# Spreading products over all 128 rows instead of 12 or 16, in a chain of two transformer blocks

## The chip, the cores and the metric

The kernel runs on one core of one Trainium2 chip, as one program in one launch. The metric is device microseconds from start to end, the median of several executions. Without the change it is 3619.73 us, the median of 3 runs (3617.62 to 3626.06).

## What is computed

Two blocks follow one another on 256 tokens of width 1024 (272 with 16 learned ones in the first block). The first block has two layers, each a SwiGLU network, a mixer and another SwiGLU network; the mixer of its first layer (the "first mixer") joins attention with a forget gate and a gated delta rule, that of its second layer is a recurrence (RWKV-7). The second block has attention, a gated linear recurrence and a retrieval layer; the change does not touch it. What matters of the reference:

```python
def forgetting_attention(q, k, v, log_f):
    c = jnp.cumsum(log_f, axis=-1)
    ...
        logits = jnp.einsum('bhqd,bhkd->bhqk', qb, k) * scale + cb[..., :, None] - c[..., None, :]
    ...
def gated_delta_rule(q, k, v, log_g, beta):
    gc = jnp.cumsum(log_g.reshape(B_, H, nc, CHUNK), axis=-1)
    decay = jnp.exp(jnp.where(causal, gc[..., :, None] - gc[..., None, :], -jnp.inf))
    kb = k * beta[..., None]
    ...
    q_dec = q * egc
    ...
def rwkv7_time_mix(h, ...):
    ...
    kk = l2_normalize((k * k_k).reshape(B_, L, H, N))
    y = rwkv7_recurrence(r_h, decay, k_h, v_h, -kk, kk * a_h)
    ...
    bonus = jnp.sum(r_h * k_h * r_k.astype(f32), axis=-1, keepdims=True) * v_h
```

Each has numbers that there are one of per head and token (the summed gates, the norms' factors, the bonus sums), and that must be applied to all the features of a head, which lie over the partitions.

## The kernel before, in words

Activations lie feature by feature over the partitions, tokens along the free axis (T = 272, in tiles of 16, 128 and 128 tokens). A weight or an activation is split into a high and a low part of a 32-bit format that TensorE takes quickly (`wload`, L77, loads through SP's DMA queue, casts `wh` on ACT at L89 and subtracts `wl` on DVE at L90), and each dense product is three (`mm3`, L114: lines L116 to L118).

A number per head and token is computed as a row, one partition per head, and is spread over the 128 partitions by a product with a selector, a matrix of zeros with ones in one row: `bcast` (L418 in the first mixer, L1064 in the recurrence) issues two, for the row's high and low part. The selectors come from an array of constants that already has 128 rows, those below the used ones zero. These are the products in question, named by the tiles that they read:

- `decay` (L517): `rowh`, `rowl` (12 rows, the summed gates) with the selector `selr`, one pair per head, 4 in all, lines L419 and L420. The rows are made in `sums` (L485).
- `scaled` (L587): `frh`, `frl` (16 rows: four factors of four heads, made in `frows`, L576), four pairs per head, 16 in all, the same lines. DVE multiplies each with keys or queries (L591).
- `attend` (L804): for each of 8 heads and 3 tiles of queries a pair that adds the keys' summed gates to the logits (L819, L820), behind products of the queries with the keys over 64 rows (L813) and one that adds the causal mask over as many rows as the tile has tokens (L815).
- In the recurrence `rows_split` (L1057) makes `rrh`, `rrl` (16 rows: the inverse norms of the keys, from `rsqrt` on DVE, L171 to L176), spread in `first` (L1271) and `unit` (L1306); `bsum` and `bsul` (16 rows, the bonus sums) are spread in `finish` (L1486). The selector there is `e2r`.

TensorE's products run in the order in which they are issued. That order follows from the generators: in the dense part of the first mixer small steps are put behind the n-th next weight block (`after`, L101, and `tick`, L105); later steps of the chains, of attention heads and of dense products take turns (`round`, L984). DVE, ACT and POOL each run theirs in order too.

Of the kernel before, what the change touches and what calls it, by code (L numbers as in the profile page):

```python
# [10 lines left out]
F32R = mybir.dt.float32r  # L11
# [321 lines left out]
class Block1(Core):  # L333
# [48 lines left out]
    def _hybrid(self, ctx, h, g):  # L382
# [15 lines left out]
        idb = ht([P, P], "idb", BF16)  # L398
        selr = ht([16, 16 * P], "selr", F32R)

        def select(q):
            w = self.wp.tile([P, 1024], F32, name=nm("w"), tag="w", bufs=WB)
            o = COFF["sel"][0] + q * 1024
            nc.sync.dma_start(w[:16], a["consts"][:16, o : o + 1024])
            V.tensor_copy(selr[:, q * 1024 : (q + 1) * 1024], w[:16])

# [10 lines left out]

        def bcast(p, rh, rl, j, n):  # L418
            M(p, selr[:n, j * P : j * P + P], rh, start=True, stop=False)  # L419
            M(p, selr[:n, j * P : j * P + P], rl, start=False, stop=True)  # L420

# [23 lines left out]
        cols, lg = ht([P, 3, 12], "cols"), ht([P, 3, 12], "lg")  # L445
        row, rowh, rowl = ht([12, T], "row"), ht([12, T], "rowh", F32R), ht([12, T], "rowl", F32R)
        em = [ht([P, 4, n], f"em{i}") for i, (_, n) in enumerate(TILES)]
# [37 lines left out]
        def sums():  # L485

            for i, (t0, n) in enumerate(TILES):
                p = psm()
                M(p[:12, :n], lg[:n, i], tri[:n, :n], start=True, stop=True)
                V.tensor_copy(row[:, t0 : t0 + n], p[:12, :n])  # L490
            c = ht([8, T], "t16")
            V.tensor_scalar(c[:, :16], row[:8, :16], -1.0, None, op0=OP.mult)
            for i in (1, 2):
                t0, n = TILES[i]
                V.tensor_scalar(c[:, t0 : t0 + n], row[:8, t0 : t0 + n], -1.0, c[:, t0 - 1 : t0], op0=OP.mult, op1=OP.add)
            V.tensor_copy(row[:8], c)
            S.copy(rowh, row)
            V.tensor_tensor(rowl, row, rowh, op=OP.subtract)
            G.memset(egc, 1.0)
            after(1, tokens)  # L500
# [16 lines left out]
        def decay(hd):  # L517

            p = psm()
            bcast(p[:, :T], rowh, rowl, 8 + hd, 12)  # L520
            for i, (t0, n) in enumerate(TILES):
                S.activation(em[i][:n, hd], p[:n, t0 : t0 + n], AF.Relu, scale=-1.0, bias=cols[:n, i, 8 + hd : 9 + hd])
            if hd == 3:
                for i, (t0, n) in enumerate(TILES):
                    S.activation(em[i][:n], em[i][:n], AF.Exp, scale=-1.0)
                    G.tensor_tensor(em[i][:n], em[i][:n], tri[:n, :n].unsqueeze(1).to_broadcast([n, 4, n]), op=OP.mult)
# [33 lines left out]

        frh, frl = ht([16, T], "frh", F32R), ht([16, T], "frl", F32R)

        def factors():
# [12 lines left out]
        def frows(fac):  # L576
            p = psm()
            for i, (t0, n) in enumerate(TILES):
                TR(p[:16, t0 : t0 + n], fac[:n, i].rearrange("p a b -> p (a b)"), ident[:n, :n])
            S.copy(frh, p[:16, :T])  # L580
            V.tensor_tensor(frl, p[:16, :T], frh, op=OP.subtract)
            for hd in range(4):
                after(1 + hd, lambda hd=hd: scaled(hd))
# [3 lines left out]
        def scaled(hd):  # L587
            for f, dst, src in ((3, kb, raw[1]), (2, kn, raw[1]), (0, qq, raw[0]), (1, qd, raw[0])):
                p = psm()
                bcast(p[:, :T], frh, frl, f * 4 + hd, 16)  # L590
                V.tensor_tensor(dst[:, hd], src[:, hd], p[:, :T], op=OP.mult)  # L591
# [212 lines left out]
        def attend(j, i):  # L804
# [11 lines left out]
            for q, p in enumerate(ps):  # L816
                hd = 2 * j + q
                s = selr[:12, hd * P : hd * P + n]
                M(p, s, rowh[:, :nk], start=False, stop=False)  # L819
# [199 lines left out]
    def _rwkv(self, ctx, h, g):  # L1019
# [16 lines left out]
        e2 = self.konst(op_, "e2")  # L1036
        e2r = ot([16, 8 * P], "e2r", F32R)
        w = self.wp.tile([P, 1024], F32, name=nm("w"), tag="w", bufs=WB)
        o = COFF["e2t"][0]
        nc.sync.dma_start(w[:16], a["consts"][:16, o : o + 1024])  # L1040
        V.tensor_copy(e2r, w[:16])

# [11 lines left out]
        gl = ot([P, 2, NT], "gl", F32R)  # L1054
        bsum = [ot([16, NT], "bsum", F32R), ot([16, NT], "bsul", F32R)]

        def rows_split(src, n):  # L1057
            x = ot([16, T], "rrh", F32R)[:, :n]
            y = ot([16, T], "rrl", F32R)[:, :n]
            S.copy(x, src)  # L1060
# [20 lines left out]
        with ExitStack() as c1:  # L1081
# [109 lines left out]
            for m in range(KT):  # L1191
# [39 lines left out]
                M(pn[:48, NM:T], e2[:, m * 80 : m * 80 + 48], rk, start=False, stop=m == KT - 1)  # L1231
            ns, rs, rt = t1([65, T], "th")[:16], t1([P, T], "ksq")[:16], t1([P, T], "kt")[:16]
            V.tensor_scalar(ns, pn[:16, :T], 1e-6, None, op0=OP.add)
            S.copy(bsum[0], pn[32:48, NM:T])
            V.tensor_tensor(bsum[1], pn[32:48, NM:T], bsum[0], op=OP.subtract)
            xv = mix(3, True)
            self.rsqrt(rs, ns, rt)
            rh, rl = rows_split(rs, T)


# [1247 lines left out]
```

## Time and profile before

| | us |
|---|---|
| median of 3 runs | 3619.73 |
| the profiled execution | 3625.6 |
| its span, first to last instruction | 3623.8 |
| PE (matmuls) busy | 3534.2 (98%) |
| PEld (weight loads) busy | 3356.2 (93%) |
| DVE busy | 2755.6 (76%) |
| ACT busy | 1932.1 (53%) |
| POOL busy | 291.8 (8%) |

PE is TensorE's matmul, PEld its load of the stationary operand, DVE VectorE, ACT ScalarE, POOL GpSimd, SP the engine whose queue issues the transfers. A form such as `12*128 12x272` is a product over 12 rows, with 128 columns of the stationary operand and 272 of the moving one. "Granted clock" is the share of TensorE's full clock, 1.00 or 0.50; its mean over the span is 0.980. Matmuls overlap, so busy PE is not PE at its peak; the distance from the start of one to the start of the next tells the pace. The first mixer runs from about 217 to 440 us, the recurrence from about 857 to 1190.

### The profile page before, as it was taken

The page shows a single profiled execution, that of the slowest core. Times are in us where ns is not written, and L with a number is a line of the kernel's source. Part 1 is how long each engine was busy: PE and PEld are TensorE (multiplying, and loading weights), DVE is VectorE, ACT ScalarE, POOL GpSimd, SP SyncE. Part 2 cuts the span into 40 slices and gives each one's busy share as a digit, 9 for nine tenths or more (in the row PEclk, how much of TensorE's full clock was granted, in tenths as well). Part 3 has the DMA queues.
Part 4 walks back from the last instruction along what each step waited for, and adds up shares of the span by engine and source line. Part 5 has one row for each costly group of instructions (what it writes and reads, how often), then busy time and mean ns, then how long its engine had stood idle before and what let it go on. Part 6 is the DMA issues. An engine that isn't in the chain of part 4 may idle for free. (4 is left out here: it accounts for less than half of the span.)

```text
span 3623.8 us, 79395 instructions
## 1 busy us (share of the span) xinstructions
PE 3534.2 (98%) x31065; PEld 3356.2 (93%) x31065; DVE 2755.6 (76%) x6245; ACT 1932.1 (53%) x4109; POOL 291.8 (8%) x380
## 2 busy tenths in 40 slices
PE   8999999999998999999999999999999999999998
PEld 8998899998887999989999999999989999997887
DVE  6677676667866877788997788657778997778866
ACT  5553455555632556655554454556765555455554
POOL 2121021110200100011000000001011000000000
PEclk9999899999997999999999999999999999999999
DMA  5551155554300565445555555555435555555554
GB/s 182 173 160 63 64 171 175 172 172 130 109 24 25 192 183 177 135 145 171 175 181 172 168 168 169 175 185 163 152 129 175 174 172 179 170 169 182 174 187 151
DMA packets 160581, 560.95 MB, mean 155 GB/s; under 512 B 18954, under 2 KB 21402, under 8 KB 160204
## 3 DMA queue, kind: packets, MB, share of 16 engines
q1 hardware_dynamic: 159788, 554.55, 47.0%
q8 instruction: 243, 3.98, 0.5%
q0 software_dynamic: 416, 1.32, 0.1%
q14 instruction: 134, 1.10, 0.1%
HBM read 554.75 MB, written 1.05 MB: 153 GB/s over the span
## 5 line engine op out<-in xcount | busy, mean ns | idle before, releaser
L89 ACT CAST wh<-w 128x512 fp32r<-128x512 f32 (+1 forms) x2102 | 1292.1, 617 | 1220.0 <-PE mm L117 723.8
L90 DVE TENSOR_TENSOR wl<-w,wh 128x512 fp32r<-128x512 f32 (+1 forms) x2102 | 1459.3, 699 | 561.2 <-ACT wh L89 530.4
L116 PE MATMUL mm<-xh,wh 128*128 128x256 f32 (+2 forms) x4032 | 1164.6, 289 | 13.4 <-ACT wh L89 12.7
L118 PE MATMUL mm<-xh,wl 128*128 128x256 f32 (+2 forms) x4032 | 1153.8, 286 | 23.2 <-DVE wl L90 23.1
L117 PE MATMUL mm<-xl,wh 128*128 128x256 f32 (+2 forms) x4032 | 1143.7, 284 | 0.9 <-DVE xl L187 0.8
L118 PEld LDWEIGHTS mm<-xh,wl 128*128 128x128 f32 x4032 | 765.9, 190 | 29.0 <-DVE wl L90 28.4
L116 PEld LDWEIGHTS mm<-xh,wh 128*128 128x128 f32 x4032 | 768.3, 191 | 17.0 <-ACT wh L89 13.6
L117 PEld LDWEIGHTS mm<-xl,wh 128*128 128x128 f32 x4032 | 769.3, 191 | 3.2 <-DVE xl L187 1.2
L2327 PE MATMUL mm<-ah,wh 128*128 128x256 f32 x768 | 218.8, 285 | 0.0
L2327 PE MATMUL mm<-al,wh 128*128 128x256 f32 x768 | 216.8, 282 | 0.0
L2327 PE MATMUL mm<-ah,wl 128*128 128x256 f32 x768 | 215.8, 281 | 0.0
L116 PE MATMUL sm<-xh,wh 128*128 128x272 f32 (+4 forms) x744 | 214.6, 288 | 0.0
L118 PE MATMUL sm<-xh,wl 128*128 128x272 f32 (+4 forms) x744 | 214.1, 288 | 0.0
L117 PE MATMUL sm<-xl,wh 128*128 128x272 f32 (+4 forms) x744 | 213.4, 287 | 0.0
L116 PE MATMUL mm<-ah,wh 128*128 128x272 f32 (+1 forms) x704 | 201.6, 286 | 0.0
L118 PE MATMUL mm<-ah,wl 128*128 128x272 f32 (+1 forms) x704 | 201.4, 286 | 0.0
L117 PE MATMUL mm<-al,wh 128*128 128x272 f32 (+1 forms) x704 | 201.2, 286 | 0.0
L2329 PE MATMUL mm<-wh,ah 128*128 128x512 f32 x384 | 153.7, 400 | 0.0
L2329 PE MATMUL mm<-wh,al 128*128 128x512 f32 x384 | 151.9, 396 | 0.0
L2329 PE MATMUL mm<-wl,ah 128*128 128x512 f32 x384 | 151.3, 394 | 0.0
L2327 PEld LDWEIGHTS mm<-al,wh 128*128 128x128 f32 x768 | 144.7, 188 | 0.2 <-DVE al L2318 0.2
L2327 PEld LDWEIGHTS mm<-ah,wl 128*128 128x128 f32 x768 | 144.8, 189 | 0.0
(877 smaller groups left out, 6640.6 us busy)
## 6 DMA issues: line engine op xcount, KB each, us to landing
w<-p_u SPq DMA_DIRECT2D x256, 512.0 KB, 3.3
w<-p_v SPq DMA_DIRECT2D x256, 512.0 KB, 3.3
w<-ffn_in SPq DMA_DIRECT2D x176, 512.0 KB, 3.3
w<-m_w_in SPq DMA_DIRECT2D x96, 512.0 KB, 3.4
w<-ffn_out SPq DMA_DIRECT2D x64, 448.0 KB, 3.3
w<-ffn_out SPq DMA_DIRECT2D x32, 512.0 KB, 3.6
w<-p_wq SPq DMA_DIRECT2D x32, 512.0 KB, 3.4
w<-hyb_w SPq DMA_DIRECT2D x28, 512.0 KB, 3.3
```

What stands on the lines that cost most here:

```text
L89: self.at_s = nc.scalar.copy(wh, w[:rows, s:e])
L90: self.at_v = nc.vector.tensor_tensor(wl, w[:rows, s:e], wh, op=OP.subtract)
L116: mm(out, wh, xh, start=start, stop=False)
L117: mm(out, wh, xl, start=False, stop=False)
L118: self.at_t = mm(out, wl, xh, start=False, stop=stop)
L2327: M(po[m // 2][:, m % 2 * T : m % 2 * T + T], w_[:, m * P : (m + 1) * P], a_, **flags)
L2329: M(po[m // 2], a_[:, i * P : (i + 1) * P], w_[:, f * 512 : f * 512 + 512], **flags)
```

## The change

Every operand of these products becomes 128 partitions high. The selectors are loaded and cast whole; the rows below the used ones of `row`, `frh`, `frl`, `rz` (which holds the inverse norms) and `bsum`, `bsul` are set to zero, by a fill on POOL and casts on ACT from the filled tile; the products drop their row limits.

```diff
-        selr = ht([16, 16 * P], "selr", F32R)
+        selr = ht([P, 16 * P], "selr", F32R)
...
-            nc.sync.dma_start(w[:16], a["consts"][:16, o : o + 1024])
-            V.tensor_copy(selr[:, q * 1024 : (q + 1) * 1024], w[:16])
+            nc.sync.dma_start(w, a["consts"][:, o : o + 1024])
+            V.tensor_copy(selr[:, q * 1024 : (q + 1) * 1024], w)
...
-        def bcast(p, rh, rl, j, n):
-            M(p, selr[:n, j * P : j * P + P], rh, start=True, stop=False)
-            M(p, selr[:n, j * P : j * P + P], rl, start=False, stop=True)
+        def bcast(p, rh, rl, j):
+            M(p, selr[:, j * P : j * P + P], rh, start=True, stop=False)
+            M(p, selr[:, j * P : j * P + P], rl, start=False, stop=True)
...
-        row, rowh, rowl = ht([12, T], "row"), ht([12, T], "rowh", F32R), ht([12, T], "rowl", F32R)
+        rows, rowh, rowl = ht([P, T], "row"), ht([P, T], "rowh", F32R), ht([P, T], "rowl", F32R)
+        row = rows[:12]
+        frh, frl = ht([P, T], "frh", F32R), ht([P, T], "frl", F32R)
+        G.memset(rows, 0.0)
+        after(5, lambda: S.copy(frh, rows))
+        after(6, lambda: S.copy(frl, rows))
...
-            S.copy(rowh, row)
-            V.tensor_tensor(rowl, row, rowh, op=OP.subtract)
+            S.copy(rowh, rows)
+            V.tensor_tensor(rowl, rows, rowh, op=OP.subtract)
...
-            S.copy(frh, p[:16, :T])
-            V.tensor_tensor(frl, p[:16, :T], frh, op=OP.subtract)
+            S.copy(frh[:16], p[:16, :T])
+            V.tensor_tensor(frl[:16], p[:16, :T], frh[:16], op=OP.subtract)
...
-                s = selr[:12, hd * P : hd * P + n]
+                s = selr[:, hd * P : hd * P + n]
...
-        e2r = ot([16, 8 * P], "e2r", F32R)
+        e2r = ot([P, 8 * P], "e2r", F32R)
...
-        nc.sync.dma_start(w[:16], a["consts"][:16, o : o + 1024])
-        V.tensor_copy(e2r, w[:16])
+        nc.sync.dma_start(w, a["consts"][:, o : o + 1024])
+        V.tensor_copy(e2r, w)
...
-        bsum = [ot([16, NT], "bsum", F32R), ot([16, NT], "bsul", F32R)]
+        bsum = [ot([P, NT], "bsum", F32R), ot([P, NT], "bsul", F32R)]
...
-            x = ot([16, T], "rrh", F32R)[:, :n]
-            y = ot([16, T], "rrl", F32R)[:, :n]
+            x = ot([P, T], "rrh", F32R)[:, :n]
+            y = ot([P, T], "rrl", F32R)[:, :n]
...
-            ns, rs, rt = t1([65, T], "th")[:16], t1([P, T], "ksq")[:16], t1([P, T], "kt")[:16]
+            ns, rz, rt = t1([65, T], "th")[:16], t1([P, T], "ksq"), t1([P, T], "kt")[:16]
+            rs = rz[:16]
+            G.memset(rz, 0.0)
+            for x in bsum:
+                S.copy(x, rz[:, :NT])
...
-            S.copy(bsum[0], pn[32:48, NM:T])
-            V.tensor_tensor(bsum[1], pn[32:48, NM:T], bsum[0], op=OP.subtract)
+            S.copy(bsum[0][:16], pn[32:48, NM:T])
+            V.tensor_tensor(bsum[1][:16], pn[32:48, NM:T], bsum[0][:16], op=OP.subtract)
...
-            rh, rl = rows_split(rs, T)
+            rh, rl = rows_split(rz, T)
```

PE's order is the same in both, instruction by instruction. ACT has four instructions more, POOL two; DVE, SP and PE have as many as before, some of them over more rows.

ACT where the norm of the keys begins in the recurrence (`wh` are weight casts, `ksq` the squared keys and then the tile of the inverse norms, `v` a value projection copied out of PSUM), before:

```order
L1212 ACTIVATE ksq_12741<-kr_12739 128x272
L89 CAST wh_12945<-w_12943 128x512
L89 CAST wh_12949<-w_12943 128x512
L1260 COPY v_2288_11236<-mm_12853 128x272
L1234 CAST bsum_11247<-acc_12094 16x256
L89 CAST wh_13029<-w_13027 128x512
```

and with the change:

```order
L1216 ACTIVATE ksq_12744<-kr_12742 128x272
L89 CAST wh_12951<-w_12949 128x512
L1240 CAST bsum_11250<-ksq_12764 128x256
L1240 CAST bsul_11251<-ksq_12764 128x256
L89 CAST wh_12955<-w_12949 128x512
L1268 COPY v_2288_11239<-mm_12859 128x272
```

The two casts that write zeros into `bsum` and `bsul` stand between the two halves of a weight block's cast.

ACT in the dense part of the first mixer (`rs` is the norm of the input, `cy` a step of a convolution), before:

```order
L161 COPY rs_2825<-sm_2965 128x272
L89 CAST wh_3081<-w_3079 128x512
L89 CAST wh_3085<-w_3079 128x512
L538 ACTIVATE cy_3017<-xpad_3014,col_2833 128x272
L89 CAST wh_3117<-w_3115 128x512
```

and with the change:

```order
L161 COPY rs_2825<-sm_2966 128x272
L89 CAST wh_3082<-w_3080 128x512
L89 CAST wh_3086<-w_3080 128x512
L451 CAST frh_2849<-row_2846 128x272
L544 ACTIVATE cy_3018<-xpad_3015,col_2833 128x272
```

The cast that clears `frh` stands ahead of a convolution step and the next weight cast; the one that clears `frl` comes a weight block later.

## Rows read from the trace of the kernel before

**Rows 1.** The page: busy time of PE, and granted clock in 40 slices.

```profile
PE 3534.2 (98%) x31065; PEld 3356.2 (93%) x31065; DVE 2755.6 (76%) x6245; ACT 1932.1 (53%) x4109; POOL 291.8 (8%) x380
...
PEclk9999899999997999999999999999999999999999
```

**Rows 2.** PE timeline around one pair of 12-row products: start, us, instruction.

```profile
268.31 0.29 PE L118 MATMUL mm<-xh,wl 128*128 128x272 f32 x1
268.53 0.39 PE L419 MATMUL sm<-rowh,selr 12*128 12x272 f32 x1
...
269.20 0.29 PE L117 MATMUL mm<-xl,wh 128*128 128x272 f32 x1
...
269.70 0.29 PE L118 MATMUL mm<-xh,wl 128*128 128x272 f32 x1
```

**Rows 3.** Instructions that read tile selr: count, duration min/median/max, forms.

```profile
L819 PE MATMUL mm<-rowh,selr x24: 165/304/591, 308.0 to 432.0; 12*16 12x16 f32 x8, 12*128 12x144 f32 x8, 12*128 12x272 f32 x8
...
L419 PE MATMUL sm<-frh,selr x16: 283/368/584, 305.9 to 311.8; 16*128 16x272 f32 x16
...
L419 PE MATMUL sm<-rowh,selr x4: 387/388/388, 268.5 to 280.9; 12*128 12x272 f32 x4
```

**Rows 4.** The same for tile e2r.

```profile
L1065 PE MATMUL sm<-rrh,e2r x16: 251/282/588, 977.8 to 1047.5; 16*128 16x16 f32 x8, 16*128 16x272 f32 x8
...
L1065 PE MATMUL sm<-bsum,e2r x16: 268/298/468, 1083.3 to 1164.8; 16*128 16x128 f32 x16
```

**Rows 5.** By stretch: busy us (count) per engine, granted clock, DMA share, GB/s.

```profile
304.40:311.20 6.80, 6.80 (x56) 5.92 (x54) 5.53 (x15) 1.56 (x3) 0.00 (x0) 1.00 0.10 37
311.20:318.05 6.85, 6.85 (x47) 6.01 (x46) 4.60 (x16) 1.18 (x5) 0.00 (x0) 0.50 0.00 0
...
338.50:345.40 6.90, 6.90 (x45) 6.36 (x45) 2.14 (x8) 2.19 (x7) 0.00 (x0) 0.51 0.00 0
...
980.20:990.50 10.30, 10.30 (x84) 8.93 (x84) 5.18 (x16) 4.13 (x12) 0.15 (x1) 0.50 0.17 55
...
1048.50:1058.70 10.20, 10.20 (x140) 8.70 (x128) 5.59 (x13) 2.44 (x5) 0.00 (x0) 0.50 0.01 2
...
1086.00:1089.50 3.50, 3.42 (x28) 2.60 (x30) 2.06 (x5) 1.20 (x2) 0.00 (x0) 0.51 0.00 0
...
1103.10:1145.00 41.90, 39.46 (x781) 35.53 (x779) 29.86 (x99) 13.59 (x32) 2.79 (x2) 1.00 0.11 35
...
1147.50:1174.80 27.30, 20.44 (x163) 18.34 (x164) 16.26 (x64) 4.23 (x13) 2.01 (x1) 0.50 0.06 20
```

**Rows 6.** The timeline of PE, products with 64-row and 128-row operands.

```profile
307.12 0.21 PE L813 MATMUL mm<-fk,fq 64*16 64x16 f32 x2
307.26 0.39 PE L419 MATMUL sm<-frh,selr 16*128 16x272 f32 x1
...
316.34 1.88 PE L606 MATMUL sm<-qq,kn 128*128 128x128 f32 x8
...
318.93 1.06 PE L606 MATMUL sm<-kb,kn 128*128 128x128 f32 x8
```

**Rows 7.** The timeline of DVE where the factors are multiplied in.

```profile
312.53 0.44 DVE L591 TENSOR_TENSOR qd<-rawq,sm 128x272 f32<-128x272 f32 x1
```

**Rows 8.** DMA issues by line: count, KB each, median us to landing.

```profile
w<-hyb_w SPq DMA_DIRECT2D x28, 512.0 KB, 3.3
...
w<-consts SPq DMA_DIRECT2D x6, 64.0 KB, 2.1
```

**Rows 9.** The timeline of SP at the second selector load.

```profile
217.56 0.37 SPq L404 DMA_DIRECT2D w<-consts  x1
```

**Rows 10.** The timeline of DVE at the second selector cast.

```profile
224.69 0.67 DVE L405 CAST selr<-w 16x1024 fp32r<-16x1024 f32 x1
```

**Rows 11.** The timeline of POOL before the norm of the keys.

```profile
967.58 0.27 POOL L1222 TENSOR_TENSOR c<-k,en 128x16 f32<-128x16 f32 x1
```

**Rows 12.** The timeline of DVE at the first step of that norm.

```profile
969.34 0.29 DVE L171 TENSOR_SCALAR ksq<-th 16x272 int32<-16x272 int32 x1
```

More of the change, by code (lines that the diff above doesn't have):

```diff
@@ L519, in decay @@
             p = psm()
-            bcast(p[:, :T], rowh, rowl, 8 + hd, 12)
+            bcast(p[:, :T], rowh, rowl, 8 + hd)
             for i, (t0, n) in enumerate(TILES):
@@ L558, in square @@
                 factors()
-        frh, frl = ht([16, T], "frh", F32R), ht([16, T], "frl", F32R)
         def factors():
@@ L589, in scaled @@
                 p = psm()
-                bcast(p[:, :T], frh, frl, f * 4 + hd, 16)
+                bcast(p[:, :T], frh, frl, f * 4 + hd)
                 V.tensor_tensor(dst[:, hd], src[:, hd], p[:, :T], op=OP.mult)
```

## The prediction

> **What bounds the kernel now.** I read the page first. TensorE's products cover 98% of the span and the granted clock is at full in nearly every slice [rows 1]; so time is won here either by making products follow one another faster or by raising the clock in the few slices below 9. Both can be looked for at the spreading products, the only ones that the change touches. Next came PE's timeline around one of them. In a dense stretch products of 272 columns start every 0.125 us (0.50 us for the four steps from 269.20 to 269.70). Around a pair over 12 rows the four steps from 268.31 to 269.20 take 0.89 us [rows 2]: 0.39 us go into entering and leaving the pair, as if the engine emptied itself each time the number of rows changes, some 0.19 us per change. The tile view then counts the products: 24, 16 and 4 that read selr and 16 and 16 that read e2r, and every one has a second with the low part beside it [rows 3, 4], 152 in all, in 33 groups of 1 to 22.
>
> The last view was busy time by stretch with the granted clock [rows 5]. From 304.4 to 311.2 us PE is busy all the time at clock 1.00, mostly with 16-row products (they run from 305.9 to 311.8 [rows 3]); then the clock is 0.50, the lower of its two levels (1.2 in place of 2.4 GHz), to 318.05, for work over 128 rows. Further falls stand right behind such groups: e2r's products begin at 977.8 and the clock is low from 980.2; they end at 1047.5, and it is low from 1048.5; those with the bonus sums begin at 1083.3, and it is low from 1086.0 [rows 4, 5]. A busy engine whose clock falls points to the rows, not to waiting: over 12 or 16 of 128 rows the array does little. That is a reading, not a proof.
>
> **The change, part by part.**
>
> *Changes of the row count.* Counted along the timeline of the products of [rows 3, 4], 35 sides of the 33 groups have a 128-row neighbour; these changes go. On 11 sides the neighbour has 16 rows (attention's short first tile, for one); there a change is new. The rest have 64-row neighbours: one change is exchanged for another. Net 24 sides; some six lie where PE waits anyway. 18 x 0.19 = 3.4 us saved. Whether a change between 64 and 128 rows costs what one between 64 and 16 does I can't read cleanly; on some 20 such sides 0.1 us either way gives bounds of 1.4 and 5.4.
>
> The products themselves keep their columns, so their streaming time; taken at nothing.
>
> A 12- or 16-row product leaves most of the array free, and 64-row products on the other half could run at the same time. At 307.26 a 16-row product follows two 64-row ones that start at 307.12, the second on the other half of the array, and it starts behind both, not with them [rows 6]; nothing is given up, and the term is 0. The Trainium skill ("TensorE: Matmul & The Clock Gate", Part 3 on packing small matmuls) says that small products in different groups of rows run concurrently, which speaks against this change; going by it the sum would be up to 2 us worse (20 sides of 0.1 us). This trace does not show it here.
>
> *The clock from 311.2 to 318.05.* If rows of zeros count as rows, the stretch before becomes full-height work and the clock should hold. Up to 312.53 DVE's last product with a factor [rows 7] holds the pace, so nothing is won. From its end, 312.97, to 318.05 PE is busy without a gap: eight products of 128 columns take 1.88 us at the low level and 1.06 at the full one [rows 6], 44% less. 5.1 x 0.44 = 2.2 us. Against the whole low stretch of 6.85 us that is a third, and a third is my price for the others, where PE is busy too but copies of other engines stand in the chain. The bounds are nothing (the copies decide) and one half (PE alone decides).
>
> *The other falls.* The stretches from 980.2 (10.3 us, 3.4 saved) and from 1086.0 (3.5 us, 1.2 saved) follow work that is mostly spreading products; I count both as held. At 338.5 (6.9 us, 2.3) and at 1048.5 (10.2 us, 3.4) the groups are smaller or PE also waits; at 1147.5 (27.3 us, up to 9) the end of the chain leaves PE idle for a quarter of the stretch (20.4 us busy [rows 5]). These I leave as they are in the sum, and give to the range.
>
> *Added work.* Three selector transfers go from 64 to 512 KB: from 2.1 us to landing to the 3.3 us of a weight [rows 8], 1.2 us each. The later of the first two is issued at 217.56 [rows 9] and cast at 224.69 [rows 10], 7.1 us on: covered; uncovered it would be 3.6 us for the three. Two zero fills on POOL and four casts on ACT are new; the two casts of frh and frl stand among weight casts in dense work, ahead of PE by the weight buffers. The tight place is the norm of the keys: POOL's last product before the fill ends at 967.85 [rows 11], and DVE's first step, which overwrites the filled tile, starts at 969.34 [rows 12]. The fill and two casts have 1.5 us. Should they need 2, DVE comes 0.5 us late, and the products at 977.8 wait for that chain. I take 0.5; bounds 0 and 2 (if the weight cast behind them is late too). Casts over 128 rows in place of 12 or 16 keep their columns: nothing.
>
> *Sum.* 3.4 + 2.2 + 3.4 + 1.2 - 0.5 = 9.7 us saved. The profiled execution took 3625.6 us, and becomes 3615.9. It lies 5.9 us above the median of the runs; against that median of 3619.73 the forecast is 3610.0 us.
>
> **The rivals.**
>
> *The clock is not held (0.18).* Either rows of zeros do not count, or the falls follow something else. Then only the first term is left: 3.4 - 0.5 = 2.9 us, 3616.8. For it: the sum rests on four falls that stand behind such groups, and after most of them PE also waits. Against it: the fall at 311.2 comes with no wait before it. The same page of the Trainium skill (Part 1, on the clock gate) has the clock go by how busy the engine has been; going by that alone PE was busy, rows would not matter, and this rival's time would come out. The rows at 311.2 differ from it.
>
> *Only the clearest stretch is held (0.15).* The groups in the recurrence are short, and the work around them has 64 rows or 16 columns; the clock may fall all the same. 3.4 + 2.2 - 0.5 = 5.1 us, 3614.6.
>
> *A fall comes earlier in the last leg of the recurrence (0.05).* From 1103.1 to 1145.0 the clock holds at 1.00 though PE is idle for 2.4 us of it [rows 5]. If the groups there run quicker and the waits behind them grow, the clock could fall at one of them and stay low to the end, as it does from 1147.5. Some 30 us more at the low level, a third of it lost, are 10 us; against the 2.9 of the first rival that ends 7.1 us slower, 3626.8. It decides only if the waits there grow past those after 1147.5 (a quarter of the time); now they are 6%. Unlikely.
>
> **How the numbers follow.** The forecast, with three stretches held or more, has 0.62 and everything in it is faster by over 0.2% (7.2 us, about what a measurement of this kernel can tell from no change). The first two rivals, 0.33, lie within 0.2%; some 0.02 of them would still come out faster when the changes of rows are worth 5.4, which makes faster 0.64, same 0.31, slower 0.05. For the range: with the stretches at 338.5 and 1048.5 held too (5.7) and two thirds of the one at 1147.5 (6) the saving is 21.4, and with 5.4 for the changes of rows 23.4: 3596. At the other end stands the first rival with its lower bound, 1.4 for the changes and 2 for the added work: 3620. I take 3597 to 3620.
>
> **What would show it right or wrong.** Right: the four steps around the pair in the dense stretch take 0.50 us; the clock is 1.00 from 304 to 318 and eight products of 128 columns then take 1.06 us; no low stretch stands behind the products at 978 and 1083; PE's order is what it was. The first rival: 0.50 us around the pair, but low stretches of the same length at the same places. Wrong altogether: the pair still takes 0.89 us (the row count is not what empties the array), a weight cast waits for one of the zero casts, or DVE waits for a selector. A single stretch more or less moves the time by 1 to 3 us, so the count of low stretches is read before the time is.

## The result, and the profile after

| | before | after |
|---|---|---|
| median, us | 3622.38 (6 runs, 3617.62 to 3626.06) | 3601.29 (6 runs, 3599.22 to 3605.21) |
| the profiled execution, us | 3625.6 | 3605.2 |
| its span, us | 3623.8 | 3603.4 |
| mean granted clock | 0.980 | 0.987 |
| low clock in the span (last stretch, at the end, left out) | 136.5 us | 85.3 us |

The ratio is 0.9944, 95% interval 0.9934 to 0.9954: 20.3 us faster by the ratio (16.7 to 23.9; the two medians are 21.1 apart), where 9.7 were forecast. A later run of the same kernel gave 3600.99 us (ratio 0.9949, 0.9937 to 0.9962).

The page of the changed kernel, busy time and granted clock in 40 slices:

```profile
PE 3508.9 (97%) x31065; PEld 3336.2 (93%) x31065; DVE 2751.2 (76%) x6245; ACT 1932.3 (54%) x4113; POOL 293.8 (8%) x382
...
PEclk9999999999999999999999999999999999999999
```

PE is busy for 25.3 us less, with as many products; the one slice at 7 [rows 1] is gone. Next comes PE's timeline around a pair with the summed gates (start, us, instruction):

```profile
268.50 0.29 PE L118 MATMUL mm<-xh,wl 128*128 128x272 f32 x1
268.63 0.29 PE L419 MATMUL sm<-rowh,selr 128*128 128x272 f32 x1
268.76 0.29 PE L420 MATMUL sm<-rowl,selr 128*128 128x272 f32 x1
268.88 0.28 PE L116 MATMUL mm<-xh,wh 128*128 128x272 f32 x1
269.00 0.29 PE L117 MATMUL mm<-xl,wh 128*128 128x272 f32 x1
```

The four steps from 268.50 to 269.00 take 0.50 us where they took 0.89 [rows 2]: the pair goes through like any dense product. The tile view of selr and that of e2r (count, duration in ns min/median/max, first and last start, forms) show all of them 128 rows high:

```profile
L823 PE MATMUL mm<-rowh,selr x24: 170/288/427, 308.4 to 422.5; 128*16 128x16 f32 x8, 128*128 128x144 f32 x8, 128*128 128x272 f32 x8
...
L419 PE MATMUL sm<-frh,selr x16: 285/372/392, 306.4 to 312.0; 128*128 128x272 f32 x16
...
L419 PE MATMUL sm<-rowh,selr x4: 286/288/288, 268.6 to 280.2; 128*128 128x272 f32 x4
...
L405 DVE CAST selr<-w x2: 673/674/676, 222.2 to 224.2; 128x1024 fp32r<-128x1024 f32 x2
```

```profile
L1069 PE MATMUL sm<-rrh,e2r x16: 256/280/392, 969.0 to 1033.9; 128*128 128x16 f32 x8, 128*128 128x272 f32 x8
...
L1069 PE MATMUL sm<-bsum,e2r x16: 273/276/328, 1068.4 to 1144.9; 128*128 128x128 f32 x16
```

Against [rows 3] the pairs in dense work fall from 387 to 288 ns; the products with the factors keep their 370 ns, since DVE sets their pace. The selector casts took the time that they took over 16 rows (0.67 us [rows 10]) and start no later.

Then the stretches of the changed kernel (a stretch at the low level is called a fall from here on): busy us (count) of PE, PEld, DVE, ACT and POOL, granted clock, DMA share, GB/s.

```profile
299.60:306.50 6.90, 6.05 (x28) 5.95 (x29) 3.65 (x11) 1.36 (x4) 0.10 (x1) 0.51 0.42 144
306.50:312.30 5.80, 5.80 (x48) 5.04 (x46) 5.38 (x16) 1.01 (x2) 0.00 (x0) 0.99 0.00 0
312.30:315.90 3.60, 3.60 (x43) 3.16 (x43) 3.22 (x15) 1.18 (x5) 0.00 (x0) 1.00 0.00 0
...
333.40:340.50 7.10, 7.10 (x80) 6.18 (x78) 3.72 (x16) 2.92 (x13) 0.00 (x0) 1.00 0.01 3
...
374.80:378.20 3.40, 3.40 (x17) 3.18 (x17) 1.96 (x9) 0.62 (x1) 0.00 (x0) 0.50 0.01 5
...
402.00:415.80 13.80, 10.95 (x51) 8.40 (x52) 6.83 (x25) 2.16 (x5) 0.00 (x0) 0.51 0.00 1
...
969.00:976.70 7.70, 7.70 (x99) 7.15 (x100) 4.95 (x18) 5.77 (x17) 1.91 (x4) 1.00 0.44 145
976.70:1037.00 60.30, 57.28 (x1432) 51.08 (x1432) 36.45 (x77) 23.21 (x60) 0.00 (x0) 1.00 0.13 40
1037.00:1043.80 6.80, 6.80 (x101) 5.90 (x100) 4.09 (x8) 1.81 (x3) 0.00 (x0) 0.50 0.01 2
...
1078.00:1088.20 10.20, 9.74 (x166) 8.69 (x167) 5.33 (x15) 2.04 (x7) 0.00 (x0) 0.50 0.01 3
1088.20:1146.20 58.00, 51.34 (x969) 45.65 (x968) 41.80 (x142) 17.09 (x42) 4.02 (x2) 1.00 0.12 38
1146.20:1156.40 10.20, 5.33 (x24) 4.96 (x25) 5.75 (x23) 1.12 (x4) 2.00 (x1) 0.50 0.01 2
```

Of the low stretches of [rows 5] three are gone: 311.2, 338.5 and 980.2. Behind the factors PE runs over 128 rows at full clock: the timeline of PE shows eight products of 128 columns in 1.06 us where they took 1.88 [rows 6].

```profile
314.98 1.06 PE L610 MATMUL sm<-qq,kn 128*128 128x128 f32 x8
```

The one at 1048.5 is shorter (6.8 us at 1037.0), so is the one at 1147.5 (10.2 us in place of 27.3). Those at 1086.0 and 1096.3 (3.4 and 6.8 us) have become one of 10.2 us at 1078.0. One is new (374.8, 3.4 us), and one that stands ahead of the factors' products, 301.0 with 3.4 us, has become 299.6 with 6.8 us.

Where the time went is read off the starts of the same product in the two timelines of PE, since PE's order did not change (one time for each kernel, from its one profiled execution):

| product | before, us | after, us | difference |
|---|---|---|---|
| L117, dense, ahead of the change | 230.04 | 229.61 | -0.43 |
| L116, dense, behind the wait for the decay's transposes | 260.12 | 260.32 | +0.20 |
| L117, behind the four pairs of `decay` | 283.08 | 282.10 | -0.98 |
| first product with the factors | 305.92 | 306.39 | +0.47 |
| behind the former stretch 311.2 | 318.05 | 315.88 | -2.17 |
| behind the former stretch 338.5 | 346.11 | 340.50 | -5.61 |
| behind the new fall at 374.8 | 385.12 | 380.32 | -4.80 |
| end of the first mixer | 440.06 | 430.55 | -9.51 |
| first product with the inverse norms | 978.09 | 969.33 | -8.76 |
| behind the former stretch 980.2 | 990.08 | 976.66 | -13.42 |
| behind the fall at 1048.5 | 1060.00 | 1045.08 | -14.92 |
| ahead of the last leg | 1145.16 | 1129.88 | -15.28 |
| behind it | 1190.07 | 1171.21 | -18.86 |
| in the second block | 1800.03 | 1779.47 | -20.56 |

The first mixer gives 9.5 us. From its end to the end of the recurrence another 9.4 come. The second block, which nothing touches, differs by 1.7 us at 1800 and by 1.5 at the end of the span; its low time is 17.0 us in both, at other places.

The added work cost one wait. PE's waits from 225 to 262 us in the kernel before (line, releaser, us in total, times, longest):

```profile
PE sm L464 <- DVE t L459: 0.8, 1, 0.8
```

and in the changed kernel:

```profile
PE sm L470 <- DVE t L465: 1.4, 1, 1.4
```

PE waits 0.6 us longer for the rows that `decay` is made of. DVE makes them behind steps of a convolution that start with `xpad` (L536, L542 in the changed kernel). Ahead of `xpad` in DVE's order stands a weight's low part, which needs ACT's cast of that weight. In ACT's timeline of the kernel before that cast comes ahead of `csq`, a step that waits for POOL:

```profile
234.94 0.62 ACT L89 CAST wh<-w 128x512 fp32r<-128x512 f32 x1
237.31 0.43 ACT L551 ACTIVATE csq<-rawq 128x272 f32<-128x272 f32 x1 [1.74 <-POOL rawq L545]
```

In the changed kernel it comes behind `csq`, and in DVE's timeline the low part waits 1.64 us for it (0.15 before):

```profile
236.35 0.43 ACT L557 ACTIVATE csq<-rawq 128x272 f32<-128x272 f32 x1 [1.56 <-POOL rawq L551]
236.68 1.12 ACT L89 CAST wh<-w 128x512 fp32r<-128x512 f32 x2
```

```profile
237.32 0.69 DVE L90 TENSOR_TENSOR wl<-w,wh 128x512 fp32r<-128x512 f32 x1 [1.64 <-ACT wh L89]
```

So `xpad` is written at 237.93 where it was at 236.56: with the two casts on ACT some of ACT's steps run in another order, though PE's do not.

The prediction's place to fear was the norm of the keys, behind the fill of `ksq`; there POOL fills at 959.03 and DVE's first step starts at 960.68, and the stretch from the last dense product (965.11 to 956.37) to the first spread one (978.09 to 969.33) is as long as it was, 12.98 and 12.96 us. No cost is seen.

### The profile page after: what moved, and what is told of

The parts are those of the page before. It is cut to its first block, busy times and chain, and to the rows that moved or that the text cites. A ratio compares the mean times of both kernels' runs of the same rounds, so it can differ in the third digit from the quotient of the medians.

```text
span 3603.4 us, 79404 instructions
## 1 busy us (share of the span) xinstructions
PE 3508.9 (97%) x31065; PEld 3336.2 (93%) x31065; DVE 2751.2 (76%) x6245; ACT 1932.3 (54%) x4113; POOL 293.8 (8%) x382
## 5 line engine op out<-in xcount | busy, mean ns | idle before, releaser
L116 PE MATMUL mm<-xh,wh 128*128 128x256 f32 (+2 forms) x4032 | 1161.8, 288 | 13.6 <-ACT wh L89 12.9
L117 PE MATMUL mm<-xl,wh 128*128 128x256 f32 (+2 forms) x4032 | 1141.7, 283 | 0.9 <-DVE xl L187 0.8
L116 PEld LDWEIGHTS mm<-xh,wh 128*128 128x128 f32 x4032 | 766.0, 190 | 16.3 <-ACT wh L89 13.8
L117 PEld LDWEIGHTS mm<-xl,wh 128*128 128x128 f32 x4032 | 767.1, 190 | 3.2 <-DVE xl L187 1.2
L116 PE MATMUL sm<-xh,wh 128*128 128x272 f32 (+4 forms) x744 | 214.8, 289 | 0.0
L117 PE MATMUL sm<-xl,wh 128*128 128x272 f32 (+4 forms) x744 | 213.6, 287 | 0.0
L116 PE MATMUL mm<-ah,wh 128*128 128x272 f32 (+1 forms) x704 | 201.6, 286 | 0.0
L117 PE MATMUL mm<-al,wh 128*128 128x272 f32 (+1 forms) x704 | 201.2, 286 | 0.0
```

The source lines that it names most:

```text
L116: mm(out, wh, xh, start=start, stop=False)
L117: mm(out, wh, xl, start=False, stop=False)
```

## The experiments

The theory after the result: what counts for the clock is how many rows of the array a product occupies, zeros included, and every us at the low level that goes is worth about a third of a us; the time lost at a change of rows is a second, smaller part. The rivals: the time comes from the changes of rows alone; or only from not leaving a group of rows; or the falls go by what the data are. "Low time" below is that of the first block in the profiled execution (119 us before, 68 with the change); a fall is given by its start and length. Each kernel has one profiled execution, so a single fall that is there or not is weaker evidence than one that agrees over several kernels.

**The first mixer alone** (`mixer`). The recurrence's part of the diff is undone (`e2r`, `bsum`, `rrh`, `rrl` and `rs` with 16 rows again, no fill there).

```diff
-        e2r = ot([P, 8 * P], "e2r", F32R)
+        e2r = ot([16, 8 * P], "e2r", F32R)
...
-            rh, rl = rows_split(rz, T)
+            rh, rl = rows_split(rs, T)
```

> The change in the first mixer alone. By the aligned start times of the same products in the two profiles, the first mixer gained 9.5 us, the recurrence 9.4, and the second block, which the change does not touch, 1.5. If the gain is made by the products where they stand (theory), this kernel is 9 to 11 us faster than before (3610 to 3614) and its low stretches in the recurrence are those of before (at about 980, 1048 and 1086 less the gain). If the gain came from falls that land elsewhere by chance (rival), the two halves don't add up: this one lies anywhere from 3602 to 3621.

Measured: 3609.12 us, ratio 0.9969 (0.9954 to 0.9984), 11 us faster. Stretches of this kernel:

```profile
303.20:333.00 29.80, 29.80 (x409) 26.57 (x408) 23.93 (x72) 7.97 (x26) 0.00 (x0) 1.00 0.13 42
...
965.40:975.60 10.20, 10.20 (x83) 8.83 (x84) 5.18 (x16) 4.13 (x12) 0.08 (x1) 0.50 0.18 55
1033.70:1043.90 10.20, 10.20 (x137) 8.81 (x129) 5.66 (x12) 2.44 (x5) 0.00 (x0) 0.50 0.01 2
```

The falls at 311 and 338 are gone, those of the recurrence at 980 and 1048 are there with the same 10.2 us each. The last leg does not follow this: with the recurrence as before it has two falls of 6.8 us (1132.7 and 1149.8) where the profile before has one of 27.3.

**The recurrence alone** (`recur`). The other half is undone (`selr`, `row`, `frh`, `frl` with 12 and 16 rows).

```diff
-        selr = ht([P, 16 * P], "selr", F32R)
+        selr = ht([16, 16 * P], "selr", F32R)
...
-                s = selr[:, hd * P : hd * P + n]
+                s = selr[:12, hd * P : hd * P + n]
```

> The change in the recurrence alone. Theory: 8 to 11 us faster than before (3610 to 3615), with the low stretches of the first mixer as before (311, 338, 397 and 410 us). Together with the kernel that has the mixer's part alone it makes up the whole (20 us). Rival as there: no such sum.

Measured: 3612.64 us, ratio 0.9977 (0.9967 to 0.9988), 8 us faster. Stretches of this kernel:

```profile
336.20:343.00 6.80, 6.80 (x43) 5.91 (x44) 2.58 (x10) 2.20 (x7) 0.00 (x0) 0.50 0.00 1
...
966.00:976.50 10.50, 10.45 (x80) 9.83 (x80) 10.05 (x24) 6.50 (x14) 0.24 (x1) 1.00 0.51 171
1141.80:1165.70 23.90, 17.61 (x144) 16.00 (x143) 12.79 (x53) 3.65 (x12) 2.01 (x1) 0.50 0.01 1
```

Here the mixer's falls stay and the one at 980 goes. Each of these goes with the products in its own place, and 11 and 8 us make up the change's 20. In the last leg the fall is 23.9 us long although the products there are 128 rows high, so its length is not shown to go by their height.

**All of it, with 32 rows** (`rows32`). The same fills, casts and products, the operands 32 rows high.

```diff
-        selr = ht([P, 16 * P], "selr", F32R)
+        selr = ht([32, 16 * P], "selr", F32R)
...
-        bsum = [ot([P, NT], "bsum", F32R), ot([P, NT], "bsul", F32R)]
+        bsum = [ot([32, NT], "bsum", F32R), ot([32, NT], "bsul", F32R)]
```

> All operands of the spreading products 32 rows high in place of 128, with the same zero fills, casts and larger transfers. Theory (height): a pair in the dense stretch still takes 0.89 us for four steps, the low stretches stand where they stood before, and the added work costs up to 1 us: 3619 to 3625, no gain. Rival (the zero rows as such, or the moved casts, made the gain): 3600 to 3605.

Measured: 3620.19 us, ratio 0.9991 (0.9981 to 1.0001): 3 us less, which can't be told from no difference. Stretches of this kernel:

```profile
310.80:317.60 6.80, 6.80 (x46) 5.98 (x46) 4.71 (x17) 1.18 (x5) 0.00 (x0) 0.50 0.00 0
338.10:344.90 6.80, 6.80 (x44) 6.15 (x44) 2.30 (x9) 2.20 (x7) 0.00 (x0) 0.50 0.00 0
976.40:986.60 10.20, 10.20 (x84) 8.83 (x84) 5.18 (x16) 4.13 (x12) 0.13 (x1) 0.50 0.16 52
```

The three falls stand where they stood. So it is neither the added work nor the longer operands as such: the height counts.

**64 rows** (`rows64`). The pairs of `decay`, `scaled` and the recurrence read 64 rows; attention's keep 128.

```diff
-            M(p, selr[:, j * P : j * P + P], rh, start=True, stop=False)
+            M(p, selr[:64, j * P : j * P + P], rh[:64], start=True, stop=False)
...
-            M(p, e2r[:, m * P : (m + 1) * P], rh, start=True, stop=False)
+            M(p, e2r[:64, m * P : (m + 1) * P], rh[:64], start=True, stop=False)
```

> The pairs of the decays, of the factors and of the recurrence over 64 rows, attention's over 128 as in the change. Theory: pairs among 128-row products change the row count again (0.89 us for four steps), those among 64-row ones don't; for the clock a 64-row product counts half, so some stretches are held and some not: 5 to 14 us faster than before, 3608 to 3617. If the clock asks only that more than 32 rows are used: 3602 to 3606. If it asks for all 128: 3612 to 3620, with the fall at 311 back.

Measured: 3614.40 us, ratio 0.9980 (0.9970 to 0.9989), 7 us faster; low time 96 us. Stretches of this kernel:

```profile
309.20:316.00 6.80, 6.80 (x45) 5.98 (x45) 4.99 (x15) 0.57 (x1) 0.00 (x0) 0.50 0.00 0
333.00:340.00 7.00, 7.00 (x116) 6.09 (x113) 4.25 (x16) 1.79 (x10) 0.00 (x0) 1.00 0.11 38
974.80:985.00 10.20, 10.20 (x84) 8.83 (x84) 5.18 (x16) 4.20 (x13) 0.00 (x0) 0.50 0.18 58
```

Behind the factors and behind the inverse norms, whose pairs have 64 rows, the clock falls as before; at 338, behind attention's pairs with 128 rows, it holds. Half the height is not enough at either place.

**Ones in the spare rows** (`ones`). The spare rows of the spread operands hold ones (those of `rowl` and `rrl`, which are differences, still zeros); the selectors' are zeros, so the sums are the same.

```diff
-        G.memset(rows, 0.0)
+        G.memset(rows, 1.0)
...
-            G.memset(rz, 0.0)
+            G.memset(rz, 1.0)
```

> The change with ones in place of zeros in the spare rows of the spread operands (the selectors are zero there, so nothing is added to a sum). Theory (only the height of a product counts, not what it multiplies): the same time as the change, 3599 to 3605, and the same low stretches within those that come and go. Rival (rows of zeros count for less in the clock): more stretches held, 3 us or more faster than the change.

Measured: 3604.24 us, ratio 0.9951 (0.9936 to 0.9966), which overlaps the change's. The clock holds where it holds with zeros (this kernel's stretch around the factors):

```profile
304.00:318.00 14.00, 14.00 (x129) 12.79 (x129) 12.63 (x37) 3.43 (x9) 0.00 (x0) 1.00 0.22 71
```

Ones or zeros in the moving operand's spare rows make no difference that these runs show; other data, and other values in the selectors, were not tried.

**The changes of rows put back** (`back`). The change, with one product over 16 zero rows and 16 columns ahead of each former group, 29 in all.

```diff
+            if low:
+                M(p[:, :16], selr[32:48, j * P : j * P + P], rh[32:48, :16], start=True, stop=True)
...
+                if q == 0:
+                    M(p[:, :16], selr[32:48, hd * P : hd * P + n], rowh[32:48, :16], start=False, stop=False)
```

> The change with one product over 16 rows and 16 columns, all zeros, ahead of each former group (34 groups or so): the changes of the row count are back, the tall products stay. It tells the two halves of the gain apart. Theory (3 us from the row counts, the rest from the clock): slower than the change by 3 to 8 us, 3604 to 3610, clock as in the change. Rival (the changes of the row count were most of it, the clock followed from them): back near before, 3615 to 3622.

Measured: 3613.56 us, ratio 0.9975 (0.9965 to 0.9986), 11 to 12 us behind the change. PE's timeline of this kernel at the first one:

```profile
269.76 0.29 PE L118 MATMUL mm<-xh,wl 128*128 128x272 f32 x1
269.98 0.27 PE L420 MATMUL sm<-rowh,selr 16*128 16x16 f32 x1
270.18 0.39 PE L421 MATMUL sm<-rowh,selr 128*128 128x272 f32 x1
270.41 0.29 PE L422 MATMUL sm<-rowl,selr 128*128 128x272 f32 x1
270.53 0.28 PE L116 MATMUL mm<-xh,wh 128*128 128x272 f32 x1
```

From 269.76 to 270.53 are 0.77 us where three steps of 0.125 would take 0.38: one short product of 16 columns costs 0.39 us, two changes. Summed over the 29 places this gives 8.0 us (it is less among 64-row products, 0.20). The other 3 to 4 us, more than had been expected in all, are the clock: a fall of 6.8 us is back at 339.7, and low time is 82 us against 68 (over all executions the mean granted clock is 0.986 to 0.989, against 0.987 to 0.990).

```profile
339.70:346.50 6.80, 6.80 (x47) 6.15 (x48) 2.50 (x10) 2.19 (x7) 0.00 (x0) 0.50 0.00 1
```

So the two parts are not independent: with more changes of rows the clock falls more often too. Whether that comes from the changes or from the short products themselves is not told apart. The rival, all of the gain in the changes of rows, does not hold either: the 311 fall stays away (the clock is 1.00 from 310 to 322 here).

**Only the factors' pairs** (`factors`) and **only attention's** (the run `attend`) are 128 rows high in the first mixer, all else as before.

```diff
-            bcast(p[:, :T], rowh, rowl, 8 + hd)
+            bcast(p[:, :T], rowh, rowl, 8 + hd, 12)
...
-                s = selr[:, hd * P : hd * P + n]
+                s = selr[:12, hd * P : hd * P + n]
```

> In the first mixer the pairs of the factors alone over 128 rows; decays and attention stay at 12, the recurrence as before. Theory: the low stretch at 311 is gone (2.2 us) with half a microsecond of row changes, and the ones at 338 and 397 stay, as the prediction had it for attention's smaller groups: 2 to 4 us faster than before, 3617 to 3620. Rival (once the clock holds there, the later falls of the mixer go too): 6 us or more, 3612 to 3615.

```diff
-            bcast(p[:, :T], rowh, rowl, 8 + hd)
+            bcast(p[:, :T], rowh, rowl, 8 + hd, 12)
...
-                bcast(p[:, :T], frh, frl, f * 4 + hd)
+                bcast(p[:, :T], frh, frl, f * 4 + hd, 16)
```

> In the first mixer attention's pairs alone over 128 rows; factors and decays as before. Theory: the fall at 311 stays (6.8 us low), the one at 338 is gone (3.3 us in the aligned profiles), and the row changes around the groups give 1 to 1.5 us; the later falls come and go: 4 to 8 us faster than before, 3614 to 3618. Rival (the prediction's reading that these groups are too small to hold the clock): the stretch at 338 stays, 1 to 2 us faster.

Measured: 3619.05 us for the factors (ratio 0.9988, 0.9979 to 0.9997, 4 us faster), 3615.97 for attention (0.9983, 0.9973 to 0.9992, 6 us). Stretches with the factors' pairs alone:

```profile
305.00:316.00 11.00, 11.00 (x96) 9.62 (x96) 8.85 (x29) 2.23 (x6) 0.00 (x0) 0.96 0.09 35
336.60:343.40 6.80, 6.80 (x44) 5.91 (x44) 2.42 (x9) 2.19 (x7) 0.00 (x0) 0.50 0.00 0
```

and with attention's alone:

```profile
310.00:316.80 6.80, 6.80 (x46) 5.97 (x46) 4.71 (x17) 1.18 (x5) 0.00 (x0) 0.50 0.00 0
337.30:340.70 3.40, 3.40 (x19) 3.15 (x20) 1.53 (x8) 1.16 (x5) 0.00 (x0) 0.50 0.00 0
```

Each fall goes by the products ahead of it: with the factors tall the one at 311 goes (the 0.96 is the tail of a fall that began at 302.4) and the one at 338 stays; with attention tall it is the other way round, but the fall at 338 is halved, not gone. With attention's pairs over 128 rows and the others over 64 or 128 it goes whole. So, as far as one execution each can tell, a fall there depends on more than the group next to it.

**Further** (`further`). The change, with the second block's 16 pairs over 8 rows and the mask products of attention's first tile (16 rows) made 128 rows high as well.

```diff
-            M(p[:, :T], selr[:8, hd * P : (hd + 1) * P], rh, start=True, stop=False)
+            M(p[:, :T], selr[:, hd * P : (hd + 1) * P], rh, start=True, stop=False)
...
-                M(p[:, t0:], idb[:n, :n], fm[:n, :n], start=False, stop=False)
+                M(p[:, t0:], idb[:, :n], fm[:, :n], start=False, stop=False)
```

> The same treatment for the 16 pairs over 8 rows in the second block and for the mask products over 16 rows in the first tile of attention. Theory: each pair among 128-row products gives back 0.39 us, 16 x 0.39 = 6.2 us, less up to 1 us for 128-row transposes and larger transfers, and 0.5 to 1 us from the mask products: 5 to 7 us faster than the change, 3594 to 3597. The clock is full around most of these pairs, so no more than one or two of the falls in the second block should go. Rival (those pairs stand where PE waits): same as the change.

Measured: 3602.41 us, ratio 0.9942 (0.9929 to 0.9956): nothing beyond the change, a miss. The pairs did quicken. That line in the changed kernel (count, duration, starts, form):

```profile
L1966 PE MATMUL sm<-rsh,selr x16: 275/382/577, 1527.8 to 2698.2; 8*128 8x256 f32 x16
```

and in this one, with PE's longest wait from 1515 to 1605 us below it:

```profile
L1966 PE MATMUL sm<-rsh,selr x16: 279/280/405, 1528.4 to 2700.2; 128*128 128x256 f32 x16
```

```profile
PE mm L118 <- DVE wl L90: 3.9, 3, 2.9
```

In the changed kernel that wait is 2.7 us there. From 2600 to 2730 us, where the second half of the pairs runs, it goes from 2.2 to 4.0. By the starts of the same products PE gains 1.8 us on the changed kernel between 1520 and 1545 us (from 0.66 behind to 1.17 ahead) and has lost it again by 1560: it waits 3.0 us longer for DVE's low part of the weights over the two places, and here the fall behind the pairs is 6.8 us long in place of 3.4. What PE gains there it spends waiting for DVE.

**Without the new wait** (`tidy`). The change, with `frh` and `frl` cleared on POOL in place of ACT, and the mask products of attention's first tile over 128 rows.

```diff
-        after(5, lambda: S.copy(frh, rows))
-        after(6, lambda: S.copy(frl, rows))
+        after(5, lambda: G.tensor_copy(frh, rows))
+        after(6, lambda: G.tensor_copy(frl, rows))
```

> The change with the two casts that clear the factor tiles on POOL in place of ACT, and the mask products of attention's first tile over 128 rows in place of 16. Theory: PE's wait for the transposes of the decays falls from 1.4 back to 0.8 us (0.6 us), and some 5 groups lose a change of the row count each (0.1 to 0.2 us, 0.5 to 1 us): 1 to 1.6 us faster than the change, at the edge of what shows, 3598 to 3602. Rival (the wait comes from elsewhere): the wait stays at 1.4 us.

Measured: 3598.08 us, ratio 0.9934 (0.9920 to 0.9947), the lowest of all. To see whether it beats the change, both ran once more on one chip, `again` being the change as it is:

> The change itself once more, as the measure for the kernel that runs beside it on the same chip. Both theories: 3601 +- 4 us, ratio 0.994 to 0.995 to the kernel before.

> The version with the two clearing copies on POOL and the first tile's mask products over 128 rows, once more, on the same chip as the change. Theory (the wait of 0.6 us that the copies on ACT cost, and the row changes around the mask products, are worth something beyond the noise): 2 to 4 us below the change, both medians on the same side in the spread. Rival (the 3 us seen before were the chip and the falls of the clock): within 1.5 us of the change.

Measured: 3600.99 us for the change, 3602.39 for this version (3594.72 to 3606.24), both 0.9949 to the kernel before (intervals 0.9937 to 0.9962 and 0.9934 to 0.9964). The 3 us did not come again. The wait did go, in both runs of it; in the second:

```profile
PE sm L470 <- DVE t L465: 0.8, 1, 0.8
```

A wait of 0.6 us less is too little to be told from the falls of the clock, which stand at other places in each execution: `again` has none at 375, where the change's first profile has one, and has one more at 1126.4. In all six profiles with every one of these products 128 rows high (the change twice, this version twice, `ones` and the version before this one) the falls at 311, 338 and 980 are gone, and low time is 58 to 68 us.

## Why the prediction was right, and where its sizes were off

*Direction and cause: right.* The forecast was 9.7 us and three stretches held or more; 20.3 us were measured, and three falls are gone, though not the same three (338.5 in place of 1086.0). 3601.29 us lies in the range of 3597 to 3620, near its fast end, and 9 us below the forecast.

*Changes of the row count: right in size.* 3.4 us were put down. The 23 groups at which the clock is full in both traces give 2.9 us together, each taken from the product ahead of it to the second one behind: 0.2 to 0.4 us for a pair of `decay`, nothing between 64-row products, up to 0.1 us lost between 16-row ones. The other ten stand in falls, where changes of rows and clock can't be told apart. (By the same timeline 36 sides have a 128-row neighbour and 19 a 64-row one, where the prediction counted 35 and some 20; that is 0.2 us.) The open price of a change between 64 and 128 rows is thus that of the change that it replaces. That small products gave up no concurrency, the term of 0, is borne out by the same sum. The Trainium skill ("TensorE: Matmul & The Clock Gate", Part 3, on packing small matmuls) would have had some loss here; these groups show none.

*The stretch at 311.2: right.* 2.2 us forecast; in the timelines the products at 312.42 before start 0.05 us later after, those at 318.05 start 2.17 us earlier. `factors` ties it to its products.

*The price of low time: right, the amount not.* The step that failed is "The other falls". It counted 20.6 us of low time as gone (311.2, 980.2 and 1086.0) and left the rest as it was, 6.8 us in the sum. Measured: 136.5 us before, 85.3 after, 51 less. Of the 20.4 us between the two spans 2.9 are changes of rows and -0.6 the added wait; 18.1 us remain for 51, a third of a us for each, the price that had been taken (1.5 of the 18.1 are from the second block, whose low time is the same in both).

The price can be checked without the change: the kernel before ran 69 times beside the experiments, with spans of 3611.9 to 3627.7 us and mean granted clocks of 0.985 to 0.979. With twice the missing share of the clock, times the span, as low time, the best straight line through them has 0.30 us of span for each us of low time (correlation 0.90). At that price 51 us are 15, an estimate, and the rest of the 20.4 would be 5 us, for the changes of rows in all 33 groups and for chance.

In single terms: 980.2 gave 4.7 us and not 3.4; 338.5, left out, gave 3.4; the falls from 396.6 to 427, of which the sum had nothing, 4.7 with their changes of rows; the last leg, 27.3 us low and now 10.2, 3.6, though `mixer` (13.7 us low there with the old recurrence) and `recur` (23.9 with the new one) don't tie this to the heights; 1048.5 gave 1.3. 1086.0, counted at 1.2, gave nothing that lasts, since a fall of 10.2 us has taken the place of it and its neighbour. A fall also came longer ahead of the factors (1.0 us lost) and a new one at 374.8 (1.3 lost).

Taking smaller groups, or waits of PE, as a reason to leave a stretch out was the error. At 338 the run `attend`, where the fall is halved, and `rows64`, where it is gone, show that it too depends on the height of attention's products, and `back`, where it returns, that it depends on the changes of rows around it. At 1048 the fall has 10.2 us in `mixer`, `attend`, `rows32` and `rows64` and 6.8 with the change and in `recur`; but `factors`, whose recurrence is as before, has 6.8 too, so that one is less sure.

*The added work: right in size, wrong in place.* 0.5 us were put at the norm of the keys, where nothing is seen. The wait is 0.6 us at the transposes for `decay`, though the text had the casts of `frh` and `frl` as covered by the weight buffers. They cover PE's own wait for weights, but not DVE's convolution, which stands behind a weight's low part, and that now waits 1.64 us for ACT's cast, whose place in ACT's order has changed. That the casts on ACT cause it is shown by `tidy`, where they are on POOL, and the wait is 0.8 us again.

*The rivals.* That the clock is not held is excluded by the stretches from 306.5 to 315.9. By the Trainium skill ("TensorE: Matmul & The Clock Gate", Part 1) the clock goes by how busy the engine was, and then rows would not matter; here PE was busy throughout ahead of 311 in both (6.80 of 6.80 us from 304.4 before, 5.80 of 5.80 from 306.5 after), and `rows32` and the change differ only in rows. That only the clearest stretch is held is excluded by 338 and 980. An earlier fall in the last leg was not seen in the profiled execution: there the clock is at 1.00 from 1088.2 to 1146.2 with PE idle for 6.7 us of it. In `again` one of 6.8 us comes at 1126.4, but the clock is full again at 1133.2 and low for only 10.2 us from 1140.1, so the cost that this rival feared did not come.

*Left open:* whether a height between 64 and 128 rows would do; what sets the length of the last leg's fall; how much of the 1.5 us in the second block, which has the same code, is chance; and why a single fall lasts 3.4 or 10.2 us.

## What to carry to other kernels

Beside a busy TensorE read the granted clock by stretch, and look at the rows of the products ahead of each fall: short ones (12 to 64 rows of 128) can lower the clock for the tall ones behind them, and padding them with zero rows was nearly free here, since the constants had the rows (0.6 us for the clearing). Price such an edit by all the low time near the products concerned, times a third (0.30 over 69 executions of this kernel), with the sure stretches as the lower bound and not as the sum. Before doing the same elsewhere see who bounds that place: in the second block PE gained 1.8 us and gave it back in waits for DVE and a longer fall.

## What the runs showed of the hardware that was not expected

Half the height is not half the effect: with 64 rows the falls at 309 and 975 are there in full length (6.8 and 10.2 us), as with 16 and 32.

One product of 16 columns over other rows costs a dense stretch 0.39 us, about three of its products of 272 columns, and with 29 of them a fall that had gone is back (low time 68 to 82 us).

Spare rows of ones and of zeros in the moving operand gave the same time (ratios 0.9951 and 0.9944, intervals overlapping).

The falls are not fixed to the program: the same kernel in two executions had 68 and 58 us of low time in its first block, which at a third of a us each is 3 of the 6 us by which its runs spread (3599.22 to 3605.21). That may be why 3 us between two versions that had not run side by side were gone once they did.
